# Two-layer hybrid encoder: the up projection of the convolution block as seven half-size block products, and its down rows placed between the up projections

## The chip, the cores and the metric

The kernel is one program for one core of a Trainium2 chip. The metric is the device time of one execution in microseconds (us). TensorE (PE in the profile, its weight loads PEld) does the products, VectorE (DVE), ScalarE (ACT) and GpSimd (POOL) the rest; the queue of SyncE (SP) issues the transfers from HBM.

## The reference, cut to what matters

```python
SEQ, D_MODEL, DEPTH, D_FF, CONV_W = 512, 1024, 2, 2816, 3

def conv_ffn(h, w_up, conv_w, conv_b, w_down):
    u = h @ w_up                                        # 512 x 1024 by 1024 x 5632
    up = jnp.pad(u, ((0, 0), (1, 1), (0, 0)))
    u = up[:, :-2] * conv_w[0] + up[:, 1:-1] * conv_w[1] + up[:, 2:] * conv_w[2] + conv_b
    gate, val = jnp.split(u, 2, axis=-1)
    return (jax.nn.silu(gate) * val) @ w_down           # 512 x 2816 by 2816 x 1024

for l in range(DEPTH):
    x = x + hybrid_mixer(rms_norm(x, norm_mix[l]), ...)           # neighbourhood and grouped-query attention
    x = x + memory_cross_attention(rms_norm(x, norm_mem_q[l]), ...)
    x = x + conv_ffn(rms_norm(x, norm_ffn[l]), w_up[l], conv_w[l], conv_b[l], w_down[l])
return rms_norm(x, norm_final)
```

All inputs and outputs are float32.

## The kernel before

Activations lie transposed in SBUF: channels on the 128 partitions, the 512 tokens along the free axis, so `xT` is eight tiles of 128x512. Products are made in the 32-bit format `float32r`, three matmuls for each: every operand is split into a rounded part `hi` and a rest `lo`, and `mm3` adds hi·hi, hi·lo and lo·hi in PSUM. Every matmul has its own weight load.

Weights pass through a stream that is written out ahead (`plan`, `plan_layer`, `plan_up`, `plan_down`). One entry is loaded by SP into a `raw` tile (two of them), `emit_split` (L728, L729) makes `hi` on ACT and `lo` on POOL, into one of four `hi` and four `lo` tiles, and `get_w` hands it to the product. A tile is used again in turn: entry n + 4 takes the place of entry n.

The convolution block of a layer has 22 pairs. Pair j is two up projections, one gate and one value block of 128 channels: 8 chunks of the 1024 inputs, times three, so 24 matmuls of 512 columns into one PSUM bank for each side. `up_finish` then multiplies both banks by the token norms (L1743, out of PSUM into SBUF), starts each convolution on ACT (L1751), adds the neighbours in four instructions a side on DVE (L1758: two of 504 columns, two of 7), and makes silu(gate)·value (L1760, L1761) and its split (L1763, L1764) into `acts[j]`. The norm's row of 512 factors stands in a PSUM bank and in an SBUF copy, `rep`.

The 22 pairs are cut into three groups (8, 7 and 7). After a group, and the first pair of the next, `down(g)` makes the eight rows of the down projection: row m takes one weight entry and as many chunks as the group has pairs, times three matmuls of 512 columns, and is added to `xT[m]` by DVE (L1787). The last group of the first layer closes each row into the next layer's norm (L910, L911, L919, L921); that of the second layer is `down_last`, in two parts, the second in halves of 256 tokens, so with matmuls of 256 columns (its additions are L1826).

PSUM has eight banks: four under the name `mm`, two `sc`, two `tr`. SBUF tiles of 128x1024 go by the name `r` (21 of them), of 128x512 by `t` (14).

The order of the instructions is not that of the text. SP's is; those of PE, ACT, DVE and POOL are chosen before the build by the class `Order`, which plays the traced program through with durations of its own, tries 30 variants, and fixes the order of the best. It may move a matmul ahead of others whose inputs are late. The order fixed, each engine runs strictly through it.

Of the kernel before, what the change touches and what calls it, by code (L numbers as in the profile page):

```python
# [19 lines left out]
P = 128  # L20
# [11 lines left out]
NF = D_FF // P  # L32
GROUPS = [(0, 8), (8, 7), (15, 7)]

LAST = [(15, 4), (19, 3)]
EPS = 1e-6
# [18 lines left out]
LATE = 3600  # L55
N_RAW, N_W, N_R, N_T, N_S, AHEAD, N_WARM, N_FIRST = 2, 4, 21, 14, 24, 2, 7, (12, 24)

# [134 lines left out]

SLOTS = {"r": N_R, "t": N_T, "s": N_S, "mm": 4, "sc": 2, "tr": 2, "raw": N_RAW, "hi": N_W, "lo": N_W, "xg": 2, "rep": 1}

# [453 lines left out]
def encoder_kernel(ctx: ExitStack, tc: tile.TileContext, t: dict, out: bass.AP):  # L648
# [17 lines left out]
    def nm(s):  # L666
        uid[0] += 1
        return f"{s}_{uid[0]}"
# [34 lines left out]
    def raw_tile():  # L703
        key, loads, nk, ncol, eng = plan[len(raws)]
        if eng[1:] == "x":
# [11 lines left out]
    def emit_split(act=ACT, cuts=2):  # L717
        n = len(ready)
        key, loads, nk, ncol, eng = plan[n]
        raw = raws[n]  # L720
        raws[n] = None
        if key[0] in ("up", "down", "memq", "memo"):
            cuts = 1
# [6 lines left out]
        ready.append((hi, lo))  # L730

    def prepare_w(ahead):

        def load():
            while len(raws) < min(len(plan), len(ready) + N_RAW):
                emit_raw()

        while len(ready) < min(len(plan), done[0] + ahead):
            load()
            emit_split()  # L740

        if woven[0]:
            late(1, load)
        else:
            load()
# [13 lines left out]

    def plan_up(l, j):  # L760
        cols(("up", j, 0), t["w_up"][l], 0, KC, P * j, P)
        cols(("up", j, 1), t["w_up"][l], 0, KC, D_FF + P * j, P)

    def plan_down(l, g):
        if (l, g) == (DEPTH - 1, len(GROUPS) - 1):
            for i, rows in enumerate(LAST):
                for mp in range(4):
                    cols(("down", "ab"[i], mp), t["w_down"][l], *rows, 256 * mp, 256)
            return
        for m in range(KC):  # L770
            cols(("down", g, m), t["w_down"][l], *GROUPS[g], P * m, P)

# [10 lines left out]
    def plan_layer(l):  # L783
# [28 lines left out]
        for mp in range(4):  # L812
            cols(("memo", 0, mp), t["w_mem_o"][l], 0, 4, 256 * mp, 256)
        for g, (j0, nj) in enumerate(GROUPS):
            for j in range(j0 + (g > 0), j0 + nj):
                plan_up(l, j)
            if g + 1 < len(GROUPS):
                plan_up(l, j0 + nj)
            plan_down(l, g)

    for l in range(DEPTH):
        plan_layer(l)

    def mm3(ps, ah, al, bh, bl, start, stop):

        PE.matmul(ps, ah, bh, start=start, stop=False)
        PE.matmul(ps, ah, bl, start=False, stop=False)
        PE.matmul(ps, al, bh, start=False, stop=stop)

# [255 lines left out]
    for l in range(DEPTH):  # L1085
# [650 lines left out]

        def up(j):
            up_finish(j, [up_project(j, side) for side in range(2)])

        def up_finish(j, us):  # L1740
            for side in range(2):
                u = tmp()
                DVE.tensor_mul(u, us[side], ffn.rep)  # L1743
                us[side] = u
            cs = []
            for side in range(2):
# [12 lines left out]
                cs.append(cc)  # L1759
            ACT.activation(cs[0], cs[0], AF.Silu)  # L1760
# [5 lines left out]
        def down(g):  # L1766
            j0, nj = GROUPS[g]
            last = g == len(GROUPS) - 1
            ops = [acts.pop(j) for j in range(j0, j0 + nj)]
            n0 = 3 if last else 0  # L1770
            opened = []
            for m in range(n0):
                pm = ps_mm()
                w = get_w(("down", g, m))
                gemm_T(pm, w, ops, range(nj - 1), 0, nj - 1)
                opened.append((pm, w))
            for m in range(KC):
                if m < n0:
# [5 lines left out]
                if last:  # L1784
                    nn.close(m, pm)
                else:
                    DVE.tensor_add(xT[m], xT[m], pm)  # L1787

# [46 lines left out]

        for g, (j0, nj) in enumerate(GROUPS):
            for j in range(j0 + (g > 0), j0 + nj):
                if j == 0:
                    up_first()
                elif j > 1:  # L1840
                    up(j)
            if g + 1 < len(GROUPS):
                up(j0 + nj)
            elif l + 1 < DEPTH:
                nn = Norm(G_MIX, l + 1)
            else:
                down_last()
                break
            down(g)

# [84 lines left out]
```

## Time and profile before

| | |
|---|---|
| time, median of 3 runs | 1334.84 us (1334.78 to 1335.59) |
| span of the profiled execution | 1334.5 us |
| what lies around the span, against the median | 0.3 us |
| instructions | 17,997 |
| PE busy | 1324.5 us, 6480 matmuls |
| PEld busy | 1112.5 us, 6480 loads |
| DVE, ACT, POOL busy | 891.5, 683.9, 707.7 us |
| bytes read from HBM | 125.65 MB, 96 GB/s over the span |

The page gives no other time for the profiled execution than its span. Busy time is that of all instructions of an engine, overlaps counted once; a group's mean is the duration of one instruction, and two instructions that follow one another on an engine can overlap in it. The chain of work that ended last goes back from the last instruction to what released it, step by step.

### The profile page before, as it was taken

Reading aid. Unit: us, or ns where it says so; the run is one execution under the profiler, and the core shown is the slowest. Engines: PE = TensorE matmul, PEld = TensorE weight load, DVE = VectorE, ACT = ScalarE, POOL = GpSimd, SP = SyncE. Lnnn points to the kernel's source line nnn. Section 1 sums busy time; section 2 is a strip of 40 time slices with the busy share of each in tenths; the row PEclk is TensorE's granted clock in tenths of the full one; section 3 lists DMA queues with packets and bytes.
Section 4 is the critical chain, followed back from the end, with each engine's and each line's share of the span. In section 5 each row is a group of like instructions: output and inputs, shape, how many; then the busy total and the mean of one; then the engine's idle time right before and its main releaser. Section 6 shows DMA issues by size and latency. Waiting matters only on the chain.

```text
span 1334.5 us, 17997 instructions
## 1 busy us (share of the span) xinstructions
PE 1324.5 (99%) x6480; PEld 1112.5 (83%) x6480; DVE 891.5 (67%) x1582; ACT 683.9 (51%) x1258; POOL 707.7 (53%) x496
## 2 busy tenths in 40 slices
PE   9999999999999999999999999999999999999998
PEld 8888888888888888888888888888888888888887
DVE  6559977675984388178535697786768825862874
ACT  6668786664442244244446687765644423432434
POOL 2667965736444444444746578664544444444443
PEclk9999999999999999999999999999999999999999
DMA  7663322323333333332355523222233333333321
GB/s 219 173 168 107 109 64 68 107 62 96 96 95 95 95 96 97 105 98 83 116 145 176 141 71 102 64 77 82 64 97 103 101 95 95 91 98 96 103 86 64
DMA packets 203705, 136.78 MB, mean 103 GB/s; under 512 B 5344, under 2 KB 193760, under 8 KB 203616
## 3 DMA queue, kind: packets, MB, share of 16 engines
q1 hardware_dynamic: 202800, 134.98, 34.3%
q8 instruction: 51, 0.84, 0.3%
q10 hardware_dynamic: 816, 0.66, 0.2%
q14 instruction: 38, 0.31, 0.1%
HBM read 125.65 MB, written 2.10 MB: 96 GB/s over the span
## 4 chain that ended last, share of the span: by engine, by line
PE 96%; DVE 2%; DMA 1%; ACT 0%; issue 0%; POOLq 0%; SPq 0%; POOL 0%; ACTq 0%
PE mm L95 84%; PE sc L95 7%; PE tr L1469 2%; PE tr L95 1%; PE tr L1314 1%; DMA raw<-in_w_in 1%; PE tr L1656 1%; DVE r L1184 0%; DVE t L1372 0%; DVE r L967 0%; PE tr L1384 0%; DMA xT<-in_xT 0%; ACT r L1182 0%; DVE t L1339 0%; DVE t L1340 0%
## 5 line engine op out<-in xcount | busy, mean ns | idle before, releaser
L729 POOL TENSOR_TENSOR lo<-raw,hi 128x512 fp32r<-128x512 f32 (+3 forms) x278 | 528.2, 1909 | 518.2 <-ACT hi L728 483.3
L95 PE MATMUL mm<-xg,hi 128*128 128x512 f32 x1728 | 534.1, 390 | 0.0
L728 ACT CAST hi<-raw 128x512 fp32r<-128x512 f32 (+3 forms) x282 | 231.8, 842 | 349.6 <-PE mm L95 271.2
L95 PEld LDWEIGHTS mm<-xg,hi 128*128 128x128 f32 x1728 | 322.6, 188 | 65.8
L95 PE MATMUL mm<-r,hi 128*128 128x512 f32 (+1 forms) x1136 | 347.9, 383 | 0.0
L95 PE MATMUL mm<-xg,lo 128*128 128x512 f32 x864 | 336.3, 389 | 0.0
L1758 DVE SCALAR_TENSOR_TENSOR t<-t,par,t 128x504 f32<-128x504 f32 (+1 forms) x352 | 285.2, 868 | 26.0 <-ACT t L1751 26.0
L95 PEld LDWEIGHTS mm<-r,hi 128*128 128x128 f32 x1136 | 209.1, 188 | 38.9
L95 PE MATMUL mm<-r,lo 128*128 128x512 f32 (+1 forms) x600 | 221.5, 372 | 0.0
L95 PEld LDWEIGHTS mm<-xg,lo 128*128 128x128 f32 x864 | 162.2, 188 | 33.9
L95 PEld LDWEIGHTS mm<-r,lo 128*128 128x128 f32 x600 | 112.9, 188 | 19.8 <-POOL lo L729 0.3
L95 PE MATMUL mm<-hi,xg 128*128 128x512 f32 (+1 forms) x384 | 111.7, 360 | 0.9 <-ACT hi L728 0.8
L1743 DVE TENSOR_TENSOR t<-mm,rep 128x512 f32<-128x512 f32 x88 | 59.7, 682 | 60.4 <-PE mm L95 44.6
L1787 DVE TENSOR_TENSOR xT<-xT,mm 128x512 f32<-128x512 f32 x32 | 21.9, 685 | 104.4 <-PE mm L95 104.4
L973 POOL TENSOR_SCALAR t<-t,s 128x512 f32<-128x512 f32 (+1 forms) x112 | 66.7, 609 | 44.4 <-DVE s L1453 23.9
L1763 ACT CAST r<-t 128x512 fp32r<-128x512 f32 x44 | 27.3, 620 | 108.4 <-DVE t L1761 108.4
L95 PEld LDWEIGHTS mm<-hi,xg 128*128 128x128 f32 x384 | 68.4, 190 | 10.2 <-ACT hi L728 1.2
L95 PE MATMUL sc<-r,r 128*128 128x256 f32 (+1 forms) x352 | 74.8, 331 | 0.0
L95 PE MATMUL mm<-lo,xg 128*128 128x512 f32 (+1 forms) x192 | 68.7, 358 | 0.0
L1751 ACT ACTIVATE t<-t,par 128x512 f32<-128x512 f32 x88 | 66.7, 806 | 1.5 <-DVE t L1743 1.5
L1447 ACT ACTIVATE t<-sc,s,qr 128x512 f32<-128x512 f32 x64 | 49.4, 777 | 23.2 <-DVE s L973 22.9
L95 PEld LDWEIGHTS sc<-r,r 128*128 128x128 f32 x352 | 53.1, 190 | 5.1
(167 smaller groups left out, 1539.1 us busy)
## 6 DMA issues: line engine op xcount, KB each, us to landing
raw<-in_w_up SPq DMA_DIRECT2D x88, 512.0 KB, 3.7
raw<-in_w_in SPq DMA_DIRECT2D x25, 512.0 KB, 4.1
raw<-in_w_down SPq DMA_DIRECT2D x24, 448.0 KB, 3.3
raw<-in_w_down SPq DMA_DIRECT2D x20, 512.0 KB, 3.6
raw<-in_w_mem_kv SPq DMA_DIRECT2D x16, 512.0 KB, 3.6
r<-in_bias SPq DMA_DIRECT2D x16, 384.0 KB, 5.2
r<-r SPq DMA_DIRECT2D x22, 256.0 KB, 5.2
raw<-in_w_in SPq DMA_DIRECT2D x18, 256.0 KB, 5.3
```

What stands on the lines that cost most here:

```text
L95: return self.engine.matmul(out, lhsT, rhs, **k)
L728: act.copy(hi[:, k], raw[:, k])
L729: (POOL if eng[0] == "P" else DVE).tensor_sub(lo[:, k], raw[:, k], f(hi)[:, k])
L973: eng.tensor_scalar(e, e, sums[:, col : col + 1], 1.0, op0=ALU.mult, op1=ALU.mult)
L1314: PE.transpose(tr[:, (2 * i + c) * P : (2 * i + c + 1) * P], es[j][:, i, c * P : (c + 1) * P], ident)
L1447: ACT.activation(e, sc[j], AF.Exp, bias=nmx[:, c], scale=qrs[b][:, col : col + 1], accum_out=sums[:, c])
L1469: PE.transpose(tr[:, k * P : (k + 1) * P], es[j][:, k * P : (k + 1) * P], ident)
L1743: DVE.tensor_mul(u, us[side], ffn.rep)
L1751: ACT.activation(cc, u, AF.Identity, bias=par[:, l, CB + ch : CB + ch + 1], scale=w[1])
L1758: DVE.scalar_tensor_tensor(cc[:, dst], u[:, src], wi, cc[:, dst], op0=ALU.mult, op1=ALU.add)
L1763: ACT.copy(acts[j][0], cs[0])
L1787: DVE.tensor_add(xT[m], xT[m], pm)
```

## The change

The blocks. For 16 of the 22 pairs of each layer the two sides of a pair, both halves of the 1024 inputs and both halves of the tokens are taken as a 2 x 2 by 2 x 2 block product, which is made with seven block products instead of eight (Strassen's scheme in its form with fifteen additions). A block product is four chunks, times three matmuls, of 256 columns. The sums of weight blocks (four of 128x512 a pair) are formed on DVE from the two loaded entries; four prepared entries (`gate`, `sums`, `diffs`, `val`) come of two loaded ones, and the `lo` parts of `sums` and `val` are made on DVE. The sums of token blocks are formed once a layer (`token_forms`, `split_tokens`), during the six pairs that stay plain. They are formed from tokens that are already multiplied by gain and norm, so the product of these pairs needs no factor afterwards. Sums of products are formed by ACT copies out of PSUM, three DVE additions in PSUM, and by further products added to a bank that has been read.

The convolution. It reads the bank itself; for plain pairs the factor is multiplied in place in PSUM (L1809 of the new kernel). The silu is written to PSUM, and the product and its split are read there.

The order of the rows. There are four groups (6, 6, 5 and 5 pairs). Two rows of the first group's down projection come ahead of the first block pair; the other rows come one or two behind each pair of the next group. The last group of each layer stays closed as before.

Room. There are three `raw` tiles, two tiles `sf` for the sums, and the program asks for a smaller scratch for transfers that are issued by software.

```diff
-GROUPS = [(0, 8), (8, 7), (15, 7)]
-LAST = [(15, 4), (19, 3)]
+GROUPS = [(0, 6), (6, 6), (12, 5), (17, 5)]
+LAST = [(17, 2), (19, 3)]
+PLAIN = 6
+FIRST_ROWS = 2
+HALF = S // 2
-N_RAW, N_W, N_R, N_T, N_S, AHEAD, N_WARM, N_FIRST = 2, 4, 21, 14, 24, 2, 7, (12, 24)
+N_SF = 2
+N_RAW, N_W, N_R, N_T, N_S, AHEAD, N_WARM, N_FIRST = 3, 4, 21, 14, 24, 2, 7, (12, 24)
...
+    def split_form(src, n, act, eng):
...
+        act.copy(hi, src)
+        eng.tensor_sub(lo, src, f(hi))
+        return hi, lo
+    def form_gate(raw, act):
+        sums["gate"] = raw
+        return split_form(raw, 4, act, POOL)
+    def form_sums(raw, act):
...
+        DVE.tensor_add(both[:, :4], raw[:, :4], raw[:, 4:])
+        DVE.tensor_sub(both[:, 4:], both[:, :4], sums["gate"][:, :4])
+        return split_form(both, 4, act, DVE)
+    def form_differences(raw, act):
...
+        DVE.tensor_sub(both[:, :4], sums["gate"][:, 4:], sums.pop("s2"))
+        DVE.tensor_sub(both[:, 4:], sums["gate"][:, :4], sums["val"][:, :4])
+        return split_form(both, 4, act, POOL)
+    def form_val(raw, act):
+        return split_form(sums["val"][:, 4:], 2, act, DVE)
...
-            while len(raws) < min(len(plan), len(ready) + N_RAW):
+            while len(raws) < len(plan) and sum(bool(e[1]) for e in plan[len(ready) : len(raws)]) < (N_RAW if woven[0] else N_RAW - 1):
...
         def up_finish(j, us):
-            for side in range(2):
-                u = tmp()
-                DVE.tensor_mul(u, us[side], ffn.rep)
-                us[side] = u
+            for u in us:
+                DVE.tensor_mul(u, u, ffn.rep)
+            convolve(j, us)
...
-            ACT.activation(cs[0], cs[0], AF.Silu)
-            DVE.tensor_mul(cs[0], cs[0], cs[1])
+            ACT.activation(us[0], cs[0], AF.Silu)
+            DVE.tensor_mul(us[0], us[0], cs[1])
             acts[j] = rpair()
-            ACT.copy(acts[j][0], cs[0])
-            DVE.tensor_sub(acts[j][1], cs[0], f(acts[j][0]))
+            split_psum(*acts[j], us[0])
...
+        def token_forms():
+            xn.extend(rtile((2, S), F32) for _ in range(4))
+            for c in range(KC):
+                DVE.scalar_tensor_tensor(xn[c // 2][:, c % 2], xT[c], ffn.gain(c), ffn.psum, op0=ALU.mult, op1=ALU.mult)
...
+            for name, a, b in (("t1", (0, 1), (0, 0)), ("t3", (1, 1), (0, 1)), ("t2", (1, 1), "t1"), ("t4", (1, 0), "t2")):
...
+                    (POOL if name == "t3" else DVE).tensor_sub(made[name][:, k], quarter(*a)[i], other)
...
+                ACT.copy(hi, src)
+                (POOL if name in ("t2", "t3") else DVE).tensor_sub(lo, src, f(hi))
+        def split_tokens():
...
+            for c, n in ((0, HALF), (2, HALF), (4, S), (6, S)):
...
+                ACT.copy(hi, src)
+                DVE.tensor_sub(lo, src, f(hi))
+        def up_forms(j):
+            a, b, c = ps_s(), ps_t(), ps_mm()
+            first, second = (v[:, halves[0]] for v in (a, c))
...
+            product(first, "gate", 0, "b11")
+            ACT.copy(p1, first)
+            product(low, "gate", 1, "b21")
+            DVE.tensor_add(low, low, p1)
+            product(second, "sums", 0, "t1")
+            ACT.copy(p5, second)
+            product(first, "sums", 1, "t2", False)
+            ACT.copy(u2, first)
+            product(second, "diffs", 0, "b22", False)
+            DVE.tensor_add(b[:, halves[1]], second, u2)
+            product(first, "diffs", 1, "t3", False)
+            DVE.tensor_add(a[:, halves[1]], first, p5)
+            product(first, "val", 0, "t4", False)
+            convolve(j, [b, a])
...
-    nc = bacc.Bacc("TRN2", target_bir_lowering=False, num_devices=1)
+    nc = bacc.Bacc("TRN2", target_bir_lowering=False, num_devices=1, dynamic_dma_scratch_size=1024)
```

More of the change, by code (lines that the diff above doesn't have):

```diff
@@ L704, in raw_tile @@
         key, loads, nk, ncol, eng = plan[len(raws)]
+        if not loads:
+            raws.append(None)
+            return None, loads
         if eng[1:] == "x":
@@ L1769, in down, with down_closing @@
+        def down(g, rows):
+            j0, nj = GROUPS[g]
+            ops = [acts[j] for j in range(j0, j0 + nj)]
+            for m in rows:
+                pm = ps_mm()
+                gemm_T(pm, get_w(("down", g, m)), ops, range(nj), 0, nj - 1)
+                DVE.tensor_add(xT[m], xT[m], pm)
+        def down_closing(g):
+            j0, nj = GROUPS[g]
             ops = [acts.pop(j) for j in range(j0, j0 + nj)]
-            n0 = 3 if last else 0
             opened = []
[L1772 to L1776, printed above, removed]
@@ L1783, in down @@
                     gemm_T(pm, get_w(("down", g, m)), ops, range(nj), 0, nj - 1)
[L1784 to L1787, printed above, removed]
+                nn.close(m, pm)
         def down_last():
@@ L1834, in down_last @@
             finish(norms[1], ys[1], True)
[L1836 to L1849, printed above, removed]
+        forms = token_forms()
+        for what, n, rows in sequence():
+            if what == "down":
+                down(n, rows)
+            elif n == 0:
+                up_first()
+            elif n > 1:
+                if n < PLAIN:
+                    next(forms, None)
+                elif n == PLAIN:
+                    for _ in forms:
+                        pass
+                    split_tokens()
+                up(n)
+        if l + 1 < DEPTH:
+            nn = Norm(G_MIX, l + 1)
+            down_closing(len(GROUPS) - 1)
+        else:
+            down_last()
     Order(tc, kept)
```

101 lines of the change are left out of this document (83 added, 18 removed).

## The prediction

> **What bounds the kernel now.** I read the page first, then the chain of waits, then the windows by stage, then the groups by shape.
>
> ```profile
> span 1334.5 us, 17997 instructions
> ...
> PE 1324.5 (99%) x6480; PEld 1112.5 (83%) x6480; DVE 891.5 (67%) x1582; ACT 683.9 (51%) x1258; POOL 707.7 (53%) x496
> ...
> PE 96%; DVE 2%; DMA 1%; ACT 0%; issue 0%; POOLq 0%; SPq 0%; POOL 0%; ACTq 0%
> ```
>
> TensorE sets the time: 96% of the chain. The chain in order of time says what one matmul costs:
>
> ```profile
> 321.68 342.76 PE mm L95 x1512
> ...
> 1320.59 4.32 PE mm L95 x36
> ```
>
> The first piece is the convolution block of layer 0, without a gap: 342.76 us / 1512 = 226.7 ns for a matmul of 512 columns. The last are 36 matmuls of 256 columns (halves of `down_last`): 120.0 ns each, 53% of the long ones and not half.
>
> ```profile
> 354.00:365.00 11.00, 11.00 (x50) 9.13 (x49) 9.83 (x14) 4.68 (x6) 4.81 (x2) 1.00 0.34 100
> 420.00:462.00 42.00, 42.00 (x187) 34.79 (x186) 7.81 (x11) 9.33 (x10) 19.10 (x8) 1.00 0.31 91
> ...
> 677.00:703.00 26.00, 26.00 (x162) 23.49 (x161) 10.14 (x16) 13.06 (x23) 11.54 (x10) 1.00 0.51 132
> 1307.00:1325.00 18.00, 18.00 (x154) 17.96 (x152) 9.98 (x28) 12.42 (x31) 6.11 (x6) 1.00 0.07 24
> ```
>
> The columns are PE, PEld, DVE, ACT, POOL busy, granted clock, DMA. In the first stretch only up projections run: DVE is busy 9.83 of 11 us. In the second, down rows alone, it is busy 7.81 of 42. The last two stretches hold most of the 256-column matmuls.
>
> **TensorE's gain.** A pair before is 2 x 24 matmuls of 512: 48 x 226.7 ns = 10.88 us. A block pair is 7 x 12 matmuls of 256: 84 x 120.0 ns = 10.08 us. That is 0.80 us for a pair, and with 16 pairs in 2 layers 25.6 us. The built programs agree on the counts: 1536 matmuls of 512 fewer, 2688 of 256 more, the others the same. Down rows keep their matmuls (22 pairs a layer, however grouped). All of this lies on the chain. A gain of 7 in 8 would be 43 us; the fixed part of a matmul (13.4 ns at 512 columns, 13.3 at 256) takes the rest.
>
> **What DVE and POOL must now do in that time.** Durations:
>
> ```profile
> L729 POOL TENSOR_TENSOR lo<-raw,hi 128x1024 fp32r<-128x1024 f32 x124 | 304.7, 2458 | 347.5 <-ACT hi L728 317.2 <-PE sc L95 30.1
> L729 POOL TENSOR_TENSOR lo<-raw,hi 128x512 fp32r<-128x512 f32 x126 | 162.7, 1308 | 89.1 <-ACT hi L728 84.5 <-issue 4.2
> L729 POOL TENSOR_TENSOR lo<-raw,hi 128x768 fp32r<-128x768 f32 x4 | 7.6, 1896 | 13.4 <-ACT hi L728 13.4
> L728 ACT CAST hi<-raw 128x1024 fp32r<-128x1024 f32 x124 | 130.4, 1053 | 259.1 <-PE mm L95 209.5 <-issue 23.2 <-POOL s L878 14.6
> L728 ACT CAST hi<-raw 128x512 fp32r<-128x512 f32 x130 | 75.5, 622 | 35.0 <-DMA raw<-in_w_in 10.9 <-PE mm L95 10.1 <-PE sc L95 6.8
> L1758 DVE SCALAR_TENSOR_TENSOR t<-t,par,t 128x504 f32<-128x504 f32 x176 | 194.0, 1121 | 26.0 <-ACT t L1751 26.0
> L1758 DVE SCALAR_TENSOR_TENSOR t<-t,par,t 128x7 f32<-128x7 f32 x176 | 103.3, 614 | 0.0
> L1751 ACT ACTIVATE t<-t,par 128x512 f32<-128x512 f32 x88 | 66.7, 806 | 1.5 <-DVE t L1743 1.5
> L1760 ACT ACTIVATE t<-t 128x512 f32<-128x512 f32 x44 | 27.6, 628 | 27.4 <-DVE t L1758 27.1
> L969 ACT ACTIVATE r<-mm,s 128x256 fp32r<-128x256 f32 x16 | 7.6, 474 | 16.8 <-PE mm L95 16.7
> L95 PE MATMUL mm<-xg,hi 128*128 128x512 f32 x1728 | 534.1, 390 | 0.0
> L1787 DVE TENSOR_TENSOR xT<-xT,mm 128x512 f32<-128x512 f32 x32 | 21.9, 685 | 104.4 <-PE mm L95 104.4
> L1826 DVE TENSOR_TENSOR xT<-xT,mm 128x256 f32<-128x256 f32 x16 | 6.7, 418 | 5.8 <-PE mm L95 5.8
> ```
>
> Some DVE instructions have far larger means than their size explains (614 ns for 7 columns). The views of single lines and tiles show why (shortest/median/longest):
>
> ```profile
> L1758 DVE SCALAR_TENSOR_TENSOR t<-t,par,t x352: 207/729/2900, 324.3 to 1293.0; 128x504 f32<-128x504 f32 x113, 128x7 f32<-128x7 f32 x63
> ...
> L1743 DVE TENSOR_TENSOR t<-mm,rep x88: 672/682/692, 322.5 to 1284.5; 128x512 f32<-128x512 f32 x88
> ...
> L921 DVE SCALAR_TENSOR_TENSOR xg<-mm,par,xg x32: 735/740/752, 235.5 to 964.9; 128x512 fp32r<-128x512 f32 x32
> ```
> ```profile
> 375.43 1.00 DVE L1758 SCALAR_TENSOR_TENSOR t<-t,par,t 128x504 f32<-128x504 f32 x3
> 376.36 0.68 DVE L1743 TENSOR_TENSOR t<-mm,rep 128x512 f32<-128x512 f32 x1
> 376.96 3.00 DVE L1758 SCALAR_TENSOR_TENSOR t<-t,par,t 128x504 f32<-128x504 f32 x2
> ```
> ```profile
> 377.10 2.84 POOL L729 TENSOR_TENSOR lo<-raw,hi 128x1024 fp32r<-128x1024 f32 x1 [2.93 <-ACT hi L728]
> ```
>
> A DVE instruction with both inputs in SBUF (`t`, `t`) waits while POOL subtracts: 376.96 to 379.96 for two of them, beside POOL's 377.10 to 379.94. Those that read PSUM (`mm`) never did, 692 and 752 ns at the longest. So the convolution out of PSUM costs 0.74 us (504 columns, by L921) and 0.21 us (7 columns, the shortest), unblocked. The three instructions at 375.43 (one of 504, two of 7) issue in 0.93 us though their durations add up to 1.15: successive ones overlap by 0.07 us.
>
> The Trainium skill (SBUF — State Buffer, Who interferes with whom) states the same as a rule: the port pair is locked for a whole instruction, and against a GpSimd instruction that reads SBUF only a DVE instruction with two SBUF inputs, or in a two-port mode, contends. It speaks for the convolution of this change and against its weight sums, which have two SBUF inputs; the trace agrees by the rows above.
>
> DVE for a block pair: convolution 4 x 0.74 + 4 x 0.21 = 3.80; product and split 2 x 0.69 = 1.38; three additions in PSUM 3 x 0.42 = 1.26; four weight sums 4 x 0.69 = 2.76; `lo` of sums (1024 columns: 0.69 and twice the step of 0.27 from 256 to 512 columns) 1.22; `lo` of val 0.69; 1.5 row additions 1.03. That is 12.1 us, less 20 overlaps, 10.7. The two multiplications by the norms (1.36) are gone. Of the 12.1 us, 4.7 (39%) have two SBUF inputs. POOL: 2 x 2.46 and 1.5 rows (768 columns 1.90; 640 columns 1.60, between 512 and 768) make 7.6 us. ACT: three casts of 1.05 and one of 0.62, 1.5 of 0.84 for the rows (768 columns, between 512 and 1024), three copies of 256 columns out of PSUM at 0.47 (L969), then 2 x 0.81, 0.63 and 0.62 from the pair: 9.3 us. PE needs 10.08 us and its rows 8 x 3 x (6 + 6 + 5) x 226.7 ns / 16 = 5.78: 15.9 us.
>
> How much of POOL's time blocks DVE? In the stretch 354 to 365 a pair (10.88 us) has 9.72 us of DVE. Unblocked it would be 2 x 0.68 + 3.80 + 1.38 less 12 x 0.07 = 5.7, so 4.0 of POOL's 4.76 us blocked it (84%), with 79% of DVE's work having two SBUF inputs. At 39% I take 39% of 7.6, 3.0 us: DVE is busy 13.7 of 15.9 us. In the first block group (one row a pair) PE's time is 14.2; DVE's there is 10.4 and 39% of 6.8, 13.1. It fits, with less to spare than in the down stretch before. The bounds are no block (10.7) and all of POOL's time (18.3).
>
> **Waits that the change adds.** Inside a pair a product adds to a bank that ACT or DVE must have read. After P1, two products (2.88 us) lie ahead of its next use; after P3 and P4, one (1.44 us) against a copy of 0.47, or 1.05 more if a cast is ahead. The narrow one is P6 to P7: DVE must add `first` into the bank's other half (0.42 us). In the built order 6 or 12 matmuls of a down row (1.36 or 2.72 us) stand between. A matmul takes 390 ns where one starts every 226.7, so its end lies 0.16 us behind its slot; with as much again for the way back, my estimate, that is 0.7 of 1.36 us. If a weight sum ahead of the addition is blocked for POOL's full 2.46, P7 is late by about 1.1 to 1.8 us, and with it everything on PE. Bounds 0 and 1.8 us a pair; the built order has 12 matmuls there where a sum stands right before the addition, in the pairs that I followed, so I take 0.05: 1.6 us in all.
>
> Weights: the view of waits has
>
> ```profile
> POOL lo L729 <- ACT hi L728: 483.3, 157, 17.0
> ACT hi L728 <- PE mm L95: 271.2, 91, 6.8
> DVE xT L1787 <- PE mm L95: 104.4, 26, 4.8
> ```
>
> so preparation waits for PE to free a slot, not PE for weights. After: the next pair's gate takes the slot of sums, free after P4, and is due after P5, P6, P7 and a row, 8.4 us, for 1.05 + 2.46. The sums have as long. The raw gate stays until both differences are made, hence a third tile; behind that wait SP holds the next loads, which have a whole pair's time. I cost this at nothing; uncovered it would be 3.5 us a pair.
>
> The token forms: per layer eight of 0.74, six of 0.69, four of 1.22 and two of 0.69 on DVE, 16.3 us, in pairs 2 to 5, where a plain pair now needs 6.6 of 10.88 us. That is hidden. Not so the end: from the last plain product to the first block product only the two early rows (8.2 us) run, and `split_tokens` may overwrite the operands only then. DVE's chain: 0.16, 0.68, ACT 0.81, 2 x 0.74 + 2 x 0.21, 0.69, cast 0.62, 0.69 = 5.6 us until pair 5's operand, needed at 5.4; then two sums, `lo` and a split of the first tokens, 3.3 us, until 8.9, needed at 9.8. POOL subtracts through all of it. If those 3.3 us stretch like the stretch 354 to 365 (9.72 / 5.7), they end at 11.2: 1.3 us late. Bounds 0 and 6 us a layer; I take 1.2, so 2.4 in all.
>
> Other stages: the third raw tile and a re-chosen order move loads and instructions there; I take 0, between -1.5 and 1.5.
>
> Sum on the profiled execution: 1334.5 - 25.6 + 1.6 + 2.4 = 1312.9 us; with the 0.3 us between span and median **1313.2 us**.
>
> **Rivals.**
>
> *Waits in most pairs.* The addition ahead of P7, or a blocked `lo`, costs 0.4 us in each pair and 3 us at each start: 12.8 + 6 against 25.6, 1328 us. For it: DVE is at 86%, its blocks come in pieces of 2.5 us. Against: before, at 89% in the up stretch, PE did not wait once. 0.15.
>
> *DVE becomes the bound (slower).* If all of POOL's time blocks it, a pair takes 18.3 instead of 15.9 us: 2.4 x 32 = 78 us, 1387 us. It decides from the point where waits reach 0.88 us a pair (25.6 + 2.7 by 32), which is 6.0 of POOL's 7.6 us blocking, 79%. For it: 84% was reached before. Against: there 79% of DVE's work was of that kind, now 39%. 0.09.
>
> *Weight loads become the bound.* PEld is busy 17.96 of 18.00 us in the last stretch and 0.83 of the time at 512 columns, so at 256 it has nothing left. At 125 ns a matmul the gain falls by 32 x 84 x 5 ns = 13.4: 1327 us; at 129.5 it is gone. Against: 36 in a row took 120.0. 0.02.
>
> *The clock drops.* If the granted clock halved in the block products, 84 x 120 ns more a pair would give 323 us: 1636. The windows' clock stays at 1.00 through the 256-column stretches, and PE has no gap in which to idle. 0.01.
> The Trainium skill (TensorE: Matmul & The Clock Gate, Why this matters for your kernels) warns that matmuls with fewer than 512 in a dimension let the clock gate close again when data is waited for; no run here shows that.
>
> *No waits, and earlier loads elsewhere help:* 1307. 0.05.
>
> **How the numbers follow.** The forecast (1308 to 1318) gets 0.68. The range 1307 to 1330 adds the case of waits in most pairs and that of weight loads; it leaves out the bound on DVE, the clock, and some of the tails. A measurement of this kernel can tell 0.2% (2.7 us) from no change. Faster than that: 0.68 + 0.05 + 0.02 and most of 0.15, 0.87; within it 0.03; slower 0.10.
>
> **What would show it.** In the profile after: 84 matmuls of 256 columns a pair at 120 ns; L1826, the new convolution, with a median of 0.73 us for 504 columns and none near 2.5; DVE about 13 to 14 us a pair; PE without gaps in the block pairs, and one or two gaps of 1 to 2 us where the plain pairs end. Wrong if PE's chain shows DVE's sums (L761 to L768) or the addition L1903 with more than 0.3 us a pair, or if the 256-column matmuls take over 122 ns.

## The result, and the profile after

| | before | after |
|---|---|---|
| median (runs) | 1334.81 us (1334.48 to 1335.59, 4) | 1323.72 us (1322.42 to 1324.98, 4) |
| span of the profiled execution | 1334.5 us | 1323.2 us |

The ratio is 0.9916, with an interval of 0.9902 to 0.9930: 11.1 us faster, where 21.6 was forecast. The time lies in the range, above the likeliest case's own range of 1308 to 1318.

The page of the new kernel: its span, the busy times, and the shares of the chain that ended last.

```profile
span 1323.2 us, 21017 instructions
...
PE 1306.0 (99%) x7632; PEld 1150.3 (87%) x7632; DVE 1004.2 (76%) x1862; ACT 783.4 (59%) x1450; POOL 724.9 (55%) x520
...
PE 91%; DVE 5%; ACT 2%; DMA 1%; issue 1%; POOL 0%; POOLq 0%; SPq 0%; ACTq 0%; DVEq 0%
```

DVE holds 5% of the chain instead of 2%, PE 91% instead of 96%. TensorE still sets the time, but not everywhere. The chain in order of time, in a block pair of layer 0:

```profile
404.05 1.44 PE mm L101 x12
405.49 1.44 PE sc L101 x12
```

Twelve matmuls of 256 columns take 1.44 us, 120.0 ns each, one product behind the other. The same view earlier, where the six plain pairs end:

```profile
377.86 1.36 DVE xg L1871
379.22 0.60 DVE r L1031
379.82 1.21 DVE r L1856 x2
...
382.01 0.74 ACT hi L749
382.76 6.68 DVE xg L1871 x2
389.44 2.28 DVE r L1856 x2
...
392.23 0.68 DVE lo L750
392.90 0.54 DVE xT L1913
393.44 0.41 DVE sc L1903
393.99 0.35 PE sc L101
```

For some 16 us the chain runs through DVE and not PE: `split_tokens` (L1871), the last sums of token blocks (L1856), a `lo` of weights, a row, and then the addition L1903 ahead of P7, which PE awaits. The windows show what that costs, and that it is confined to this place (columns: PE, PEld, DVE, ACT, POOL busy, granted clock, DMA):

```profile
385.00:391.00 6.00, 5.93 (x44) 5.60 (x45) 6.00 (x3) 1.31 (x3) 6.00 (x3) 1.00 0.01 3
391.00:394.50 3.50, 1.13 (x8) 0.76 (x7) 3.50 (x6) 1.99 (x2) 0.25 (x2) 1.00 0.08 19
394.50:400.00 5.50, 5.50 (x25) 4.94 (x26) 4.88 (x9) 1.40 (x2) 2.71 (x1) 0.69 0.56 155
395.66:399.06 3.40, 3.40 (x15) 3.11 (x14) 2.83 (x5) 0.78 (x1) 1.55 (x1) 0.50 0.58 172
400.00:410.00 10.00, 10.00 (x78) 9.66 (x77) 8.16 (x16) 7.24 (x12) 6.11 (x3) 1.00 0.49 141
410.00:620.00 210.00, 210.00 (x1461) 196.79 (x1460) 180.53 (x280) 113.35 (x168) 97.46 (x47) 1.00 0.34 99
424.50:438.70 14.20, 14.20 (x103) 13.45 (x103) 12.53 (x22) 8.05 (x12) 6.75 (x4) 1.00 0.36 103
1030.00:1050.00 20.00, 16.48 (x107) 14.95 (x107) 18.93 (x17) 7.75 (x11) 11.81 (x4) 0.94 0.25 73
1047.61:1051.00 3.39, 3.39 (x15) 3.00 (x14) 2.21 (x5) 1.74 (x3) 0.00 (x0) 0.50 0.58 171
```

From 385 to 391 us DVE works on three instructions and completes two. Then PE idles for 2.4 of 3.5 us, and behind that its clock is granted at half (0.50) for 3.4 us, until 399.06; the 0.69 of the longer row is a mean over stretches at 0.50 and at 1.00. Layer 1 shows the same (1030 to 1050, with the clock at half until 1051). From 410 to 620 us PE has no gap in 210 us.

The timeline of DVE, that of POOL, and the group by shape of the subtractions of 1024 columns (busy, mean ns):

```profile
382.08 7.37 DVE L1871 TENSOR_TENSOR xg<-r,xg 128x512 fp32r<-128x512 f32 x3
389.37 2.94 DVE L1856 TENSOR_TENSOR r<-r,r 128x512 f32<-128x512 f32 x2
392.23 0.68 DVE L750 TENSOR_TENSOR lo<-raw,hi 128x512 fp32r<-128x512 f32 x1
```
```profile
382.19 2.83 POOL L1859 TENSOR_TENSOR r<-r,r 128x1024 fp32r<-128x1024 f32 x1 [3.52 <-ACT r L1858]
384.98 3.38 POOL L750 TENSOR_TENSOR lo<-sf,hi 128x1024 fp32r<-128x1024 f32 x1
388.32 2.83 POOL L741 TENSOR_TENSOR lo<-raw,hi 128x768 fp32r<-128x768 f32 x1
```
```profile
L1871 DVE TENSOR_TENSOR xg<-r,xg 128x1024 fp32r<-128x1024 f32 x2 | 6.8, 3420 | 0.0
```

An instruction of 1024 columns takes 3.42 us here. Both engines have both inputs in SBUF and a queue of work, and they take turns: POOL to 385.0, DVE's second subtraction to 386.1, POOL's second to 388.4, DVE's third to 389.4, POOL's third to 391.2, DVE's sum to 391.7. Each of the three blocked DVE instructions pays a whole POOL instruction, and POOL pays too (3.38 us for 1024 columns, where L729 of the kernel before has 2.46). Three instructions of 1.22, 1.22 and 0.68 us, 3.1 us in all, take 9.0. The Trainium skill (SBUF — State Buffer, Who interferes with whom) says that of two such instructions the later one blocks fully until the other's is over; these rows agree, and show that with both queues full it does so once per instruction.

Where the 11.1 us come from can be counted. Take as pace 226.7 ns from one start to the next after a matmul of 512 columns, 120 after 256, 109 after 128 and 60 after one column, and add up by how much starts in the trace are later than that (earlier ones count against it). This is time that PE lost, to waits and to a low clock above all (us, profiled execution; the last four columns are stages of layer 0 and, from 1020 on, of layer 1):

| kernel | whole | 0–150 | 370–412, plain pairs end | 412–640, block pairs | 640–670, layer ends | 1020–1050, plain pairs end |
|---|---|---|---|---|---|---|
| before | 16.5 | 6.4 | 0.0 | 0.0 | 0.1 | 0.0 |
| after | 30.8 | 8.8 | 5.2 | 0.5 | 0.5 | 5.4 |
| rows4 | 27.4 | 11.1 | 1.0 | 0.5 | 3.5 | 0.0 |
| forms_early | 27.1 | 9.2 | 1.7 | 0.5 | 0.4 | 2.6 |
| forms_dve | 28.9 | 8.7 | 4.5 | 0.5 | 0.5 | 3.1 |
| early_rows4 | 24.3 | 9.0 | 0.0 | 0.5 | 4.7 | 0.0 |
| plain_all | 18.5 | 8.7 | 0.0 | 0.0 | 0.0 | 0.0 |
| rows_block | 41.0 | 8.7 | 0.0 | 8.4 | 1.7 | 0.0 |
| rows4_psq | 22.6 | 9.1 | 1.5 | 0.5 | 0.5 | 0.0 |
| early_rows4_psq | 19.8 | 9.0 | 0.1 | 0.5 | 0.5 | 0.0 |
| before_raw3 | 18.7 | 9.1 | 0.0 | 0.0 | 0.0 | 0.0 |
| best_two_loads | 18.7 | 8.2 | 0.1 | 0.5 | 0.5 | 0.0 |

After against before: 14.3 us more lost. The matmuls' 25.6 less 14.3 is 11.3, the difference of the spans (1334.5 - 1323.2); this has to come out, since the 25.6 are worked out with the same paces. What the table shows is where the loss lies. The block pairs from 412 to 640 us lose 0.5 us against a pace of 120 ns, so the products brought what was forecast, and 10.6 of the 14.3 were given back in two places, once a layer.

### The profile page after: what moved, and what is told of

It is laid out like the page before. It is cut to its first block, busy times and chain, and to the rows that moved or that the text cites. A ratio compares the mean times of both kernels' runs of the same rounds, so it can differ in the third digit from the quotient of the medians.

```text
span 1323.2 us, 21017 instructions
## 1 busy us (share of the span) xinstructions
PE 1306.0 (99%) x7632; PEld 1150.3 (87%) x7632; DVE 1004.2 (76%) x1862; ACT 783.4 (59%) x1450; POOL 724.9 (55%) x520
## 4 chain that ended last, share of the span: by engine, by line
PE 91%; DVE 5%; ACT 2%; DMA 1%; issue 1%; POOL 0%; POOLq 0%; SPq 0%; ACTq 0%; DVEq 0%
PE mm L101 62%; PE sc L101 21%; PE tr L101 4%; PE tr L1533 2%; DVE xg L1871 1%; PE tr L1378 1%; DVE r L1856 1%; DMA r<-in_bias 1%; DVE r L1031 1%; PE tr L1720 1%; DMA raw<-in_w_in 0%; ACT t L1356 0%; DVE r L1248 0%; DVE sc L1350 0%; ACT r L1227 0%
## 5 line engine op out<-in xcount | busy, mean ns | idle before, releaser
L741 POOL TENSOR_TENSOR lo<-raw,hi 128x512 fp32r<-128x512 f32 (+3 forms) x230 | 371.3, 1629 | 291.2 <-ACT hi L740 243.5
L101 PE MATMUL mm<-xg,hi 128*128 128x512 f32 (+1 forms) x960 | 266.5, 363 | 0.5 <-ACT t L1897 0.3
L101 PEld LDWEIGHTS mm<-xg,hi 128*128 128x128 f32 x960 | 170.5, 189 | 27.3 <-issue 1.0
L101 PE MATMUL mm<-xg,lo 128*128 128x512 f32 (+1 forms) x480 | 173.5, 361 | 0.0
L101 PE MATMUL sc<-r,hi 128*128 128x256 f32 (+1 forms) x832 | 165.9, 294 | 5.7 <-DVE sc L1903 5.0
L750 POOL TENSOR_TENSOR lo<-sf,hi 128x1024 fp32r<-128x1024 f32 x32 | 79.1, 2473 | 140.2 <-ACT hi L749 117.0
L101 PEld LDWEIGHTS mm<-r,lo 128*128 128x128 f32 x728 | 137.9, 189 | 19.8
L101 PEld LDWEIGHTS sc<-r,hi 128*128 128x128 f32 x832 | 135.6, 193 | 12.2 <-issue 3.1
L101 PE MATMUL sc<-r,lo 128*128 128x256 f32 (+1 forms) x416 | 122.0, 293 | 0.0
L749 ACT CAST hi<-sf 128x1024 fp32r<-128x1024 f32 x64 | 67.1, 1050 | 78.8 <-DVE sf L762 46.3
L750 POOL TENSOR_TENSOR lo<-raw,hi 128x1024 fp32r<-128x1024 f32 x32 | 78.1, 2439 | 47.9 <-ACT hi L749 32.9
L101 PEld LDWEIGHTS mm<-xg,lo 128*128 128x128 f32 x480 | 90.6, 189 | 14.2 <-POOL lo L750 0.2
L101 PEld LDWEIGHTS sc<-r,lo 128*128 128x128 f32 x416 | 80.4, 193 | 1.3
```

The source lines that it names most:

```text
L101: return self.engine.matmul(out, lhsT, rhs, **k)
L741: (POOL if eng[0] == "P" else DVE).tensor_sub(lo[:, k], raw[:, k], f(hi)[:, k])
L749: act.copy(hi, src)
L750: eng.tensor_sub(lo, src, f(hi))
```

## The experiments

Two theories stood for the 10.6 us: that PE has too little work ahead of the first block product while DVE's forms and splits come due together (the place), or that every block pair would lose time in some form and the first one only shows it (the pair's own waits).

**rows4: four early rows instead of two.**

```diff
-FIRST_ROWS = 2
+FIRST_ROWS = 4
```

> Four instead of two down rows ahead of the first block pair; all else as in the changed kernel. Theory (the time lost lies where the plain pairs end: VectorE, blocked by GpSimd, is about 5 us late with the token blocks there, and the clock then halves for some 2 us): 16.3 instead of 8.2 us of down rows cover it, both gaps go, PE's excess near 375 to 400 and 1025 to 1050 us falls from 10.6 to under 2 us, time about 1314 to 1316. Rival (the lost time is VectorE's load over all block pairs, and only came to light there): the later pairs have fewer rows beside them, so the wait moves into them and the time stays at 1322 to 1325 or grows.

Measured: 1315.95 us (1315.55 to 1321.3), ratio 0.9865 (0.9849 to 0.9881), 7.8 us less than the changed kernel. The place loses 1.0 and 0.0 us instead of 5.2 and 5.4; the window in which its first block products lie shows the clock kept:

```profile
400.00:410.00 10.00, 9.54 (x76) 9.01 (x75) 8.90 (x14) 5.60 (x9) 2.43 (x2) 1.00 0.32 93
```

That settles for the place. The profiled execution is the slowest of the four, 1321.3; of that, 3.5 us stand at the end of layer 0 and 11.1 in the first 150 us. Each of these two stages holds a fall of the clock to half (76.5 to 79.9 and 667.0 to 670.4 us), worth some 1.7 us each (half of 3.4). The mean granted clock of this execution is 0.995 and that of the other three 0.997 to 0.998, so falls of the clock seem to be part of the 5 us by which executions of this kernel differ; what the rest is, and why they fall in one execution and not in another, stays open.

**forms_early: the sums of token blocks called for sooner.** The sums take `r` tiles in the order of the program's text, and the last two of the four were traced behind pair 5's result. The edit calls two steps at pair 3 and two at pair 4, so that none is left behind pair 5.

```diff
-                    next(forms, None)
+                    for _ in range((0, 0, 1, 2, 2, 1)[n]):
+                        next(forms, None)
```

> The four token sums are called for one or two pairs earlier, so that all of them are allotted room ahead of pair 5's result; only the splits of the token blocks themselves are left where the plain pairs end. Same instructions. Theory (backlog of VectorE at that place, 6 of its about 13 us there being sums t2 and t4): the two gaps shrink to under 1 us each, time about 1314 to 1316. Rival (the splits alone, which must wait for the last plain product, are enough to make the wait): a gap of 2 us or more stays in each layer, 1318 to 1322.

Measured: 1320.99 us (1320.01 to 1321.29), ratio 0.9891 (0.9876 to 0.9906). The place loses 1.7 and 2.6 us. A window of it, and the wait that is left:

```profile
385.00:388.00 3.00, 2.37 (x20) 2.16 (x19) 3.00 (x5) 1.50 (x4) 0.38 (x1) 1.00 0.06 16
```
```profile
PE tr L101 <- DVE xg L1871: 2.0, 4, 0.8
```

So 6.3 of the 10.6 us hung on sums that were late, with the clock's fall behind them; the rest are the splits themselves. The clock stays at 1.00 here, with no wait over 0.8 us. The time came out in the rival's range, though: only 2.7 us less than the changed kernel. In the profiled execution 2.4 of the 6.3 us are lost again between 670 and 1020 us, ahead of layer 1's convolution block (6.7 us instead of 4.3, counted the same way); why is not known.

**forms_dve: the token sums and their rests on DVE alone.** If POOL's subtraction of a token block is what blocks DVE, DVE should be better off doing it.

```diff
-                    (POOL if name == "t3" else DVE).tensor_sub(made[name][:, k], quarter(*a)[i], other)
+                    DVE.tensor_sub(made[name][:, k], quarter(*a)[i], other)
...
-                (POOL if name in ("t2", "t3") else DVE).tensor_sub(lo, src, f(hi))
+                DVE.tensor_sub(lo, src, f(hi))
```

> All sums and rests of the token blocks on VectorE, none on GpSimd (two sums and two rests a layer move, 4.8 us of VectorE's time for 7.5 us of GpSimd's). Theory A (VectorE is late since GpSimd blocks it): fewer blocks, so VectorE's three subtractions L1871 take 1.2 us each and not 2.4 to 3.3, the gaps shrink though VectorE has more to do, 1317 to 1321. Theory B (VectorE has too much work there, blocked or not): the gaps grow by up to 4.8 us a layer, 1325 to 1333.

Measured: 1325.28 us (1322.34 to 1325.46), ratio 0.9919 (0.9906 to 0.9931): no difference from the changed kernel. The block is gone from the three subtractions (L1871), but the sums (L1856) now have it, by the groups in this stretch, and PE waits all the same, by the view of waits and the windows:

```profile
L1871 DVE TENSOR_TENSOR xg<-r,xg 128x1024 fp32r<-128x1024 f32 x2 | 2.4, 1220 | 0.0
L1856 DVE TENSOR_TENSOR r<-r,r 128x512 f32<-128x512 f32 x6 | 7.7, 1316 | 0.0
```
```profile
PE sc L101 <- ACT r L1858: 3.2, 1, 3.2
```
```profile
384.00:390.00 6.00, 2.79 (x21) 2.28 (x19) 6.00 (x5) 2.08 (x3) 2.96 (x2) 1.00 0.01 3
390.00:394.00 4.00, 3.54 (x27) 3.21 (x27) 4.00 (x5) 1.90 (x4) 0.98 (x1) 1.00 0.42 126
```

DVE is busy throughout. Part of what it lost to POOL it now does itself, and some 3.8 us of block are left: six sums of 1.32 us on average, where an unblocked one takes 0.68. The place loses 7.6 us instead of 10.6. So theory A had the subtractions right and the time wrong, and the run does not separate the block from the amount of DVE's own work: both make DVE late at this place. That the clock stays at 1.00 behind a wait of 3.2 us was not expected.

**early_rows4: both remedies.** FIRST_ROWS = 4 and the sums called for sooner.

> Both: token sums earlier and four rows ahead of the first block pair. If the place where the plain pairs end is all that was lost against the sum of the matmuls, this comes to 1313 to 1314 and no lower, since either alone removes most of it; if each leaves a rest, it is lower than both by 1 to 2 us.

Measured: 1318.61 us (1318.12 to 1320.55), ratio 0.9878 (0.9865 to 0.9892). The place loses nothing any more, in either layer, but 4.7 us are lost at the end of layer 0. There DVE's last addition of squares (two inputs in SBUF) meets a run of POOL's subtractions; the timelines of DVE and POOL, and the row of the view of waits:

```profile
657.72 4.39 DVE L1002 TENSOR_TENSOR t<-t,t 128x512 f32<-128x512 f32 x1 [0.77 <-ACT t L991]
662.03 0.74 DVE L985 SCALAR_TENSOR_TENSOR xg<-mm,par,xg 128x512 fp32r<-128x512 f32 x1
```
```profile
656.50 5.07 POOL L741 TENSOR_TENSOR lo<-raw,hi 128x512 fp32r<-128x512 f32 x4
```
```profile
PE sc L101 <- DVE xg L985: 2.4, 1, 2.4
```

One addition of 0.69 us takes 4.39. It does not get its turn after the first subtraction: POOL goes on from one to the next, and DVE comes when the four are through, at 661.6. The norm behind it (L985) makes PE wait 2.4 us, and behind the wait the clock stands at half, by the windows:

```profile
664.10:667.40 3.30, 3.30 (x10) 2.72 (x10) 1.51 (x5) 0.53 (x2) 1.40 (x1) 0.50 0.39 113
```

The expected 1313 to 1314 us were missed for a reason outside the theory.

**plain_all: no block products.** PLAIN = 22: all pairs plain, no token forms and no room for the tiles `sf`; groups, order of rows, convolution from PSUM, the tiles of `raw` and the smaller scratch stay.

```diff
-PLAIN = 6
+PLAIN = 22
...
-                if n < PLAIN:
-                    next(forms, None)
-                elif n == PLAIN:
+                if n == PLAIN:
```

> No block products: all 22 pairs of a layer as two plain projections of 512 columns; the four groups, the rows between the pairs and the convolution out of PSUM stay. Theory (the whole gain comes from the 256-column products, 0.80 us for each of 32 pairs, and the rest of the change is worth nothing by itself because VectorE was hidden before): within 1.5 us of the kernel before, 1333 to 1337. Rival (the rows or the convolution out of PSUM bring part of the gain): 1325 to 1330.

Measured: 1340.21 us (1337.97 to 1342.13), ratio 1.0034 (1.0021 to 1.0046): 4.9 us slower than before, a miss on the slow side. The rest of the change brings no time; it costs some. The block products by themselves bring 1340.2 - 1323.7 = 16.5 us, after what the place takes back. In the trace the loss lies in the first 150 us, which the block products do not touch; what of it remains between this execution and the median is not attributed.

**rows_block: the rows in a block again.** All eight rows of a group ahead of the next group's first pair, none between the pairs; the block products stay. This takes away the matmuls that lie between P6 and P7.

```diff
-            at = FIRST_ROWS if g == 1 else 0
-            if at:
-                yield "down", 0, range(at)
+            if g > 0:
+                yield "down", g - 1, range(KC)
...
-                if g > 0:
-                    to = at + (KC - at) * (i + 1) // nj if g == 1 else KC * (i + 1) // nj
-                    yield "down", g - 1, range(row, to) if i else range(at, to)
-                    row = to
```

> Block products as in the changed kernel, but all eight down rows of a group stand together ahead of the next group's first pair, none between pairs. Theory (VectorE has room for a pair only because 5.8 us of rows lie beside each): a pair by itself is 10.1 us for PE and 10 us plus some 2 us of blocks for VectorE, so PE waits 1 to 2 us a pair and P6 to P7 has only the next pair's products for cover; the gap where the plain pairs end goes (32 us of rows cover it). 20 to 50 us more within the pairs, 10 less at the start: 1333 to 1365. Rival (VectorE would fit anyway, the place of the rows matters only at the start): 1313 to 1316.

Measured: 1333.87 us (1331.16 to 1335.39), ratio 0.9984 (0.9975 to 0.9994): 18 us more than rows4. The place loses nothing here either; the view of waits and a window in the block pairs:

```profile
PE sc L101 <- ACT t L1888: 12.0, 12, 1.5
```
```profile
425.00:460.00 35.00, 33.21 (x274) 32.80 (x274) 34.75 (x60) 21.71 (x34) 14.41 (x6) 1.00 0.30 88
```

With a pair in 10 us DVE is busy 34.75 of 35 us, and PE waits in 12 pairs. It waits not on the addition ahead of P7 but on ACT's copy of P1 (L1888), queued behind activations whose DVE inputs are late. So the rows between the pairs are what the block products need, less for the matmuls between P6 and P7 than for DVE's time. In the trace, counted the same way, the block pairs lose 8.4 us in layer 0 and 8.5 in layer 1, less than the 20 to 50 expected of the pairs.

**rows4_psq and early_rows4_psq: the last square in PSUM.** If the end of layer 0 is lost to the block of L1002, an addition with one input in PSUM must not lose it. The last square of each norm over all tokens goes to a free PSUM bank, once in rows4 and once in early_rows4.

```diff
-            sq = tmp((self.n,)) if self.gcol is not None or c == 0 or c >= KC - 2 else ps_s()[:, : self.n]
+            if self.gcol is not None and c == KC - 1 and self.n == S:
+                sq = ps_t()[:, : self.n]
+            else:
+                sq = tmp((self.n,)) if self.gcol is not None or c == 0 or c >= KC - 2 else ps_s()[:, : self.n]
```

> Four early rows, and the last square of each norm that is summed on VectorE is written to a PSUM bank, so that this addition has one input in SBUF. Theory (that addition, at the end of a layer, waits for several of GpSimd's subtractions on end, and PE for it): PE's excess near 650 us goes from 3.7 to about 0.5, 1312 to 1316. Rival (the wait there is the chain of the norm itself): unchanged against four early rows alone, 1316.

> The same with the token sums called for earlier. Theory: the addition that took 4.4 us takes 0.7, the excess near 650 us goes from 4.8 to about 0.5, 1313 to 1315. Rival: 1318 to 1319.

Measured: rows4_psq 1317.07 us (1315.99 to 1317.39), ratio 0.9861 (0.9847 to 0.9874), where 1312 to 1316 was expected and rows4 has 1315.95; early_rows4_psq 1314.64 us (1313.86 to 1316.9), ratio 0.9847 (0.9834 to 0.9860). In the second the same addition, now at L1005, stands beside the same run of subtractions, by the timelines of DVE and POOL:

```profile
658.13 0.68 DVE L1005 TENSOR_TENSOR t<-t,tr 128x512 f32<-128x512 f32 x1
```
```profile
656.27 5.04 POOL L741 TENSOR_TENSOR lo<-raw,hi 128x512 fp32r<-128x512 f32 x4
```

0.68 us instead of 4.39, and the stage loses 0.5 instead of 4.7: the block was the cause there. In rows4_psq the stage's loss fell as well, from 3.5 to 0.5, and the time did not follow; the 3.5 had been read in the slowest execution of rows4, and its median need not hold them.

**before_raw3: the kernel before with the new loading.** Three `raw` tiles, three loads ahead during attention, the smaller scratch; nothing else of the change.

```diff
-N_RAW, N_W, N_R, N_T, N_S, AHEAD, N_WARM, N_FIRST = 2, 4, 21, 14, 24, 2, 7, (12, 24)
+N_RAW, N_W, N_R, N_T, N_S, AHEAD, N_WARM, N_FIRST = 3, 4, 21, 14, 24, 2, 7, (12, 24)
...
-            while len(raws) < min(len(plan), len(ready) + N_RAW):
+            while len(raws) < min(len(plan), len(ready) + (N_RAW if woven[0] else N_RAW - 1)):
...
-    nc = bacc.Bacc("TRN2", target_bir_lowering=False, num_devices=1)
+    nc = bacc.Bacc("TRN2", target_bir_lowering=False, num_devices=1, dynamic_dma_scratch_size=1024)
```

> The kernel before with the change's room and loads alone: three raw tiles, up to three loads ahead in the attention stages, the smaller scratch; no block products, no moved rows. Theory (PE's excess of some 2.5 us in the first 150 us, and the 4.9 us by which all-plain pairs with the new order were slower than before, come from the loads and the order chosen around them): 2 to 5 us slower than before, 1337 to 1340. Rival (they come from the rows between the pairs and the convolution): 1335, as before.

Measured: 1338.36 us (1336.28 to 1340.35), ratio 1.0022 (1.0013 to 1.0031), 3.2 us slower. The first 150 us lose 9.1 us instead of 6.4. So the loss there, in the changed kernel and in plain_all, comes with the loading and the order chosen with it. Which of the two was not separated.

**best_two_loads and best_other_order.** Both start from early_rows4_psq. The first keeps the loads in attention to two ahead; the second only starts the search for an order from another seed (4 to 5), to see how much of all these differences is luck of the search.

```diff
-            while len(raws) < len(plan) and sum(bool(e[1]) for e in plan[len(ready) : len(raws)]) < (N_RAW if woven[0] else N_RAW - 1):
+            while len(raws) < len(plan) and sum(bool(e[1]) for e in plan[len(ready) : len(raws)]) < N_RAW - 1:
```

> The fastest kernel so far (token sums earlier, four early rows, last square in PSUM) with two loads ahead in the attention stages as before, not three; three raw tiles stay. Theory (the third load in the attention stages costs the excess there): the excess in the first 150 us falls from 9.0 to about 6.5 us, 1311 to 1313. Rival (a matter of the chosen order): within 2 us of 1314.6 either way.

> The fastest kernel so far with another seed for the search of the instruction order; nothing else. Theory (what is left against the sum of the matmuls is the luck of the search, a few us): 1312 to 1319. Rival (the order found hardly matters): within 0.7 us of 1314.6.

Measured: best_two_loads 1313.02 us (1312.88 to 1313.11), ratio 0.9833 (0.9820 to 0.9847), 22.2 us (1335.2 - 1313.0) faster than before and 10.7 faster than the changed kernel, the fastest of all. best_other_order 1315.03 us (1314.28 to 1317.01), ratio 0.9851 (0.9837 to 0.9864), 0.4 from its twin: the one other seed tried changed little here. Every edit above also has a newly chosen order, and the seed was not varied in the changed kernel itself, so differences of about a microsecond are not read as effects. The first 150 us recovered 0.8 us (9.0 to 8.2), not the 6.5 us level expected; two loads ahead are not the whole of that loss, and the rival (within 2 us of 1314.6) fits the time too. The span of best_two_loads, and its block pairs in layer 0:

```profile
span 1311.1 us, 21014 instructions
```
```profile
384.00:620.00 236.00, 236.00 (x1668) 222.36 (x1667) 206.73 (x316) 127.56 (x192) 112.75 (x53) 1.00 0.35 100
```

From the first block pair of layer 0 to 620 us PE is busy without a gap at full clock. This kernel loses 2.2 us more than before over the whole (18.7 against 16.5): 25.6 - 2.2 = 23.4, the difference of the profiled spans (1334.5 - 1311.1).

## Why the prediction was right, and where it was not

The direction and the range held; the gain was half of the one forecast. That 1323.7 us lies in the range is in part luck: the likeliest case ended at 1318, and the range went on to 1330 for waits in most pairs (1328) and for weight loads (1327), neither of which came.

**The matmuls, 25.6 us: right.** 1.44 us for twelve, no gap from 410 to 620 us, and 0.5 us lost against that pace in layer 0's block pairs.

**P6 to P7, 1.6 us: too much.** The waits of the addition's line:

```profile
L1903 DVE TENSOR_TENSOR sc<-sc,t x32: 419/432/433, 393.4 to 1275.4; 128x256 f32<-128x256 f32 x32
...
  PE sc L101: 14.8, 18
...
  PE sc L101: 5.0, 2
```

The first of the two waits is DVE's for PE, 18 times; the last PE's for DVE, twice in 32 pairs, both in the first block pair of a layer, so they belong to the next term. Elsewhere it cost nothing.

**The convolution and DVE's load: right.**

```profile
L1826 DVE SCALAR_TENSOR_TENSOR t<-tr,par,t x128: 206/474/745, 396.6 to 1277.3; 128x504 f32<-128x504 f32 x64, 128x7 f32<-128x7 f32 x64
```

None of them was blocked: 745 ns at the longest, and the same for those that read `sc` and `mm`. DVE was busy 180.5 of 210 us, 86%, where 13.7 of 15.9 is 86%; in the pair of the first block group 12.53 of 14.2 us where 13.1 was worked out. The block came out about as taken, on the average: from 410 to 620 us the fourteen additions L761 took 1.90 us each and the fourteen `lo` of L750 with 512 columns 1.69, where an unblocked one takes 0.68; with the late ones among L767, DVE spent some 35 us more than unblocked, 36% of POOL's 97.5 us, where 39% was taken. Preparation of weights cost nothing, as said: in the changed kernel's view of waits no matmul waits for it by more than 0.2 us.

**The place where plain pairs end, 2.4 us: the term that was mis-sized; it measured 10.6.** 5.2 and 5.4 us lie within the bounds of 0 to 6 a layer; the value taken, 1.2, was far too small (the working had given 1.3). Three things in it were off. (1) The sums were counted as done in pairs 2 to 5; of layer 0's, four of 0.68 us and two rests (`lo`, L1859) were still out at 379.7 us. Calling for them sooner returned 6.3 us in this place. All four splits (3.8 us unblocked) also stood ahead of L1903 in DVE's order, where one was counted, so that PE's long wait was for that addition in the first block pair and not for an operand. (2) The block was taken as a factor of 1.7, from a stretch in which POOL had work for 4.81 of 11 us. Here POOL worked without a break, and three DVE instructions of 3.1 us took 9.0, a factor of 2.9. A mean over a stage did not hold for the one place where both queues were full. (3) PE's wait of 2.3 us was followed by 3.4 us at half the clock, which the term did not have. PE's timeline there:

```profile
397.34 0.63 PE L101 MATMUL sc<-r,hi 128*128 128x256 f32 x2
397.77 0.41 PE L101 MATMUL sc<-r,lo 128*128 128x256 f32 x1
397.98 0.63 PE L101 MATMUL sc<-r,hi 128*128 128x256 f32 x2
```

Three matmuls start in 0.64 us, 213 ns apart instead of 120; half of 3.4 us is 1.7 of layer 0's 5.2 us. The clock's rival had supposed an idle PE and rejected it; the idle PE was in another term of the same sum.

**Other stages, 0 (±1.5): missed.** The first 150 us lost 2.4 us more. The kernel before, given the new loading alone, lost 3.2 us: an edit costed at nothing without naming what covers it in attention.

**The 0.3 us between span and median: wrong reading.** Each execution of these two kernels lies 1.7 to 1.8 us above its own span (1324.98 and 1323.2; 1322.42 and 1320.6; before, 1335.62 and 1333.8). The profiled span of before, 1334.5, therefore belongs to an execution some 1.4 us longer than the median. The forecast of the difference is not touched by it.

**The rivals.** Waits in most pairs did not come (0.5 us lost in all between 412 and 640 us), nor did weight loads set the pace (PEld busy 196.8 of 210 us, and 120 ns a matmul), nor did DVE become the bound; it does with the rows out of the pairs (rows_block). That best_two_loads ends at 1313.02, beside the forecast 1313.2, is no proof of the forecast: it has mended losses that the prediction had partly counted and partly not.

## What to carry to other kernels

Where a faster product moves work to DVE, add up each engine's work at the seam between two schemes, not over a stage: here the 16 pairs of layer 0 lost 0.5 us in all, and the seam, once a layer, took back 40% of the gain. For an instruction with two SBUF inputs beside a POOL whose queue is full, reckon with one whole POOL instruction per instruction, or a whole run of them, unless one input can stand in PSUM. Put movable TensorE work (four rows instead of two) at such a seam, and call for what it needs before the allocation order makes it late.

## What the runs showed of the hardware that was not expected

- A DVE addition waited through the rest of a run of four POOL subtractions (4.39 us for 0.69), where elsewhere the two engines alternated instruction by instruction. With one input in PSUM it took 0.68 us beside the same run. What decides between taking turns and waiting out the run was not tried.
- The clock fell behind short waits: to half for 3.4 us after 2.3 us of idle PE in the changed kernel. After a wait of 3.2 us in forms_dve it stayed at 1.00. The Trainium skill (TensorE: Matmul & The Clock Gate, HAM oscillation — how this bites in real kernels) gives gaps of more than about 3.4 us as the abstract rule; here a shorter one was followed by a drop and a longer one, still under the rule's figure, was not, so in these runs the length of the gap alone does not tell.
- Where a wait lies in time counts as well. Within a trace the falls begin whole multiples of 3.413 us apart: the changed kernel's at 395.65 and 1047.60 by 191.0 of them, those of rows4 at 76.48 and 666.98 by 173.0. Cut into steps on that grid, the 2.3 us wait leaves PE 1.8 us idle in the one step that ends at 395.65, while the 3.2 us wait of forms_dve lies across an edge at 386.43, with some 1.6 us in each step:

```profile
392.24:395.65 3.41, 1.62 (x9) 1.33 (x9) 3.38 (x7) 1.99 (x2) 1.24 (x1) 1.00 0.40 97
```
```profile
383.02:386.43 3.41, 1.86 (x16) 1.65 (x14) 3.41 (x3) 0.69 (x2) 2.78 (x1) 1.00 0.00 0
386.43:389.85 3.42, 1.77 (x13) 1.61 (x13) 3.42 (x4) 1.94 (x3) 1.01 (x1) 1.00 0.02 5
```

In the thirteen traces, from 20 us on and ahead of the last 20 us, every step with more than 1.7 us of idle PE was followed by a fall (four, at 1.8 to 2.7), and none with less than 1.2. Between 1.2 and 1.7 us both occurred, so the idle time in a step is not the whole rule either, and no run varied it by itself.
